# Forgetting attention: the values of a head in one run of 64-column products instead of two mixed runs

## The chip, the core and the metric

The kernel runs on one core of one Trainium2 chip. Time is device time in microseconds (us) of one launch; the kernel before takes 1184.59 us as the median of three runs (1183.14 to 1188.25). One further execution was recorded by the hardware profiler; its rows are what is read below. TensorE is called PE there (PEld is its weight load), VectorE DVE, ScalarE ACT, GpSimd POOL, and SyncE SP, whose queue issues most DMAs.

## The reference

Two layers on x of 1024 tokens by 1024 features. Layer 0 mixes a causal pooling branch with a cross-attention into 256 memory tokens; layer 1 mixes forgetting attention (16 heads of 64 features) with the same kind of memory attention. Each layer ends with a gated output projection, a residual and a LayerNorm. The change concerns the forgetting attention, cut here to its core:

```python
logits = einsum('bqhd,bkhd->bhqk', q, k) * scale + (cum_q - cum_k)
logits = where(kpos <= qpos, logits, -inf)
p = softmax(logits, axis=-1)
out = einsum('bhqk,bkhd->bqhd', p, v)          # "the values"
y = concat([out * silu(g_main), y_mem * silu(g_mem)]) @ w_out
```

## The kernel before, in words

All arithmetic that needs float32 accuracy is done with split operands: a number is a high part and a low part in 16 bits, and a product is the sum of three matmuls (high by high, high by low, low by high).

Layer 1's attention runs in the function `fox`. It goes through 16 heads, and in each through eight steps, one for each tile of 128 queries, the largest tile first: step 0 takes tile 7 (1024 keys wide, since the mask is causal), step 7 takes tile 0 (128 keys). A step has these parts on PE, in an order that the program fixes by hand: the logits of the tile (L323, one or two PSUM banks of the ring "L"), then a share of "fill" (the projections of queries, keys, values and gates for the heads to come, L359, whose columns are handed out so that the steps are equally long), then, in some steps, the values of older tiles (L1130), then the rest of the fill. On DVE the mask and the minimum are taken of the logits (L1068), on ACT the exponential (L1076), then ACT and DVE make the high and low halves of the probabilities (L1104 and L1105), and a transposing DMA from the SP queue (L1121) turns them, so that keys lie on the partitions. Tiles 3 and 2 go in one such DMA, and so do tiles 1 and 0. The turned tiles lie in six buffers of the tag "T".

Values are taken by `values(hd, c, o)`, six steps (LAG) behind the last of four tiles: tiles 7 to 4 (c = 1) in step 1 of the next head, tiles 3 to 0 (c = 0) in its step 5. A call has two parts. "Highs" take the high half of the probabilities with 128 stationary columns (the high and the low part of v side by side), 26 matmuls for c = 1 and 10 for c = 0. "Lows" take the low half with only the high part of v, which is 64 columns; two of them stand side by side in the array and write to the two halves of the partitions. c = 1 does its lows first, c = 0 its highs. The result lies in two halves of the partitions that must be added: ACT scales one half into the output tile `o` (L1148), DVE multiplies and adds the other (L1149). The bank is one of the four of the ring "L", which the logits use too. The table VALUES tells the fill how many columns the two steps spend on values, 39 and 15 blocks of 128.

After the second head of a pair, `pair_out` multiplies by the gate on POOL (L1158), right behind each call of `values`, and after c = 0 stores the pair to DRAM from the SP queue (L1160). The POOL queue also holds the masks of coming tiles (L1042) and the splitting of weights (L176, L193, L178).

The rest of the kernel uses the same eight PSUM banks: four "L", two "pj" (projections) and two "T" (exponentials, transposes).

Of the kernel before, what the change touches and what calls it, by code (L numbers as in the profile page):

```python
# [9 lines left out]
F32 = mybir.dt.float32  # L10
F32R = mybir.dt.float32r
BF16 = mybir.dt.bfloat16
F16 = mybir.dt.float16
# [25 lines left out]
QKSCALE = 2.0 ** -17  # L39
VALUES = {1: 39 * P, 5: 15 * P}  # L40

# [37 lines left out]
def trunk_kernel(ctx, tc, x, xT, memT, win, wk, wv0, wv, wmk, wmv, wout, poolw, pscale, lng, lnb, bforget, out):  # L79
# [15 lines left out]
    nc.vector.memset(warm, 0.0)  # L95
    idle = psum.tile([P, NH], F32, tag="L", name="idle", bufs=4)
    for _ in range(9):
# [30 lines left out]
    def w_slots(tags, where):  # L128

        def tiles(k):  # L130
            tag, bufs = tags[k]
            if tag == "w":
                return [parts_of(wt, [P, NH]) for _ in range(2)]
            two, four = [P, 2, NH], [P, 2, 2, NH]
            if tag == "MK":
                hi, pair = MK(two), MK(four, BF16)
            elif tag == "PG":
# [323 lines left out]
    def mem_attention(l, X, kv, qtile, ytile, yd, behind=None, before=None, last=None):  # L461
# [12 lines left out]
        if l:  # L474
            with tc.manual_schedule(engines={PE}):
                one, two = queries(0, ("L", 4)), queries(1)
# [19 lines left out]
        def probs(i):  # L496

            p, two = sb([P, MH, NMEM], "P", 4), sb([P, 2, MH, NMEM], "P", 4, F16)
            m, ms, sm, r = tiny(MH), tiny(MH), tiny(MH), tiny(MH)
            for hp in range(2):  # L500
                lg = ps([P, 2, NMEM], "L", 4)
                for n, j in ((0, 0), (0, 1), (1, 1), (2, 1), (1, 0), (2, 0)):
                    h = 2 * hp + j
                    a, b = three(qs[h][:, i * P : (i + 1) * P], mk[:, h, :])[n]
                    nc.tensor.matmul(lg[:, j, :], a, b, start=(n, j) == (0, 0), stop=(n, j) == (2, 0))
                pair = slice(2 * hp, 2 * hp + 2)
                nc.vector.tensor_reduce(m[:, pair], lg, AX.X, ALU.max, negate=True)
                nc.vector.tensor_scalar(ms[:, pair], m[:, pair], MSCALE, None, ALU.mult)
                for j in range(2):
                    h = 2 * hp + j  # L510
                    nc.scalar.activation(
                        p[:, h, :], lg[:, j, :], AF.Exp, bias=ms[:, h : h + 1], scale=MSCALE, accum_out=sm[:, h : h + 1],
                    )
            nc.vector.tensor_scalar(r, sm, 1.0 / PSCALE, None, ALU.mult)
            nc.vector.reciprocal(r, r)
            for h in range(MH):
                nc.scalar.activation(two[:, 0, h, :], p[:, h, :], AF.Copy, scale=r[:, h : h + 1])
                nc.vector.scalar_tensor_tensor(
                    two[:, 1, h, :], p[:, h, :], r[:, h : h + 1], two[:, 0, h, :], ALU.mult, ALU.subtract,
                )  # L520
            pt[i] = T([P, 2, MH, 2, P], F16)
            nc.sync.dma_start_transpose(
                pt[i].rearrange("p e h m q -> p (e h m) q"), two.rearrange("p e h t -> p (e h t)"),
            )

        def values(c, h):
            acc = ps([P, NH], *(("L", 4) if h == 1 else ("T", 2)))
            for j in range(4):
# [31 lines left out]
    class OutProj:  # L560
# [34 lines left out]

        def open(self, banks=(("L", 4), ("pj", 2)) * 2):
            accs = [ps([P, NH], *bank) for bank in banks]
            return accs[:2], accs[2:]
# [44 lines left out]
        def rest(self, resid, X, dst):  # L643
# [14 lines left out]
            for sp, c in order:  # L658
                if c == 2:
                    accs[sp] = self.open((("T", 2), ("T", 2), ("L", 4), ("L", 4))) if 0 in accs and sp == 1 else self.open()  # L660
                if self.begun and (sp, c) == (0, 0):
# [76 lines left out]
    with tc.tile_pool(name="in0", bufs=1) as in0:  # L738
# [34 lines left out]
        def pool_group(g, see=None):  # L773
            w = WINDOWS[g]
            pms = []
            for f in (2 * g, 2 * g + 1):
                u = sb([P, S], "P", 4)
                run(slab(
                    first[f] if g == 0 else win[0, f], X, lambda cols, acc: nc.scalar.copy(u[:, cols], acc),
                    ("L", 4) if f == 1 else ("pj", 2),  # L780
                ))
# [23 lines left out]
            for d in range(2):  # L805
                f = 2 * g + d
                for n in range(2):
                    acc = ps([P, NH], *(("pj", 2) if d and n else ("L", 4)))
                    terms = []
# [26 lines left out]
    with tc.tile_pool(name="in1", bufs=1) as in1:  # L836
# [9 lines left out]
        def vt(shape, dt=F32R):  # L846
            return sb(shape, "V", 4, dt, in1)

# [54 lines left out]
        def forget_gates():  # L903
# [23 lines left out]
            yield  # L927
            ca = ps([P, 2 * P], "L", 4)
            nc.tensor.matmul(ca[:, :n], tri, lf, start=True, stop=False)
# [122 lines left out]
        def probs(hd, i, R, sums, inverse, behind):  # L1052
# [11 lines left out]
            for n, (lo, up) in enumerate(parts):  # L1064
                lg = ps([P, NH], "L", 4)[:, : up - lo]
                mm3(lg, ((q[:, qs], kx[:, lo:up]), (q[:, qs], ky[:, lo:up])))
# [40 lines left out]

        pt = {}

        def turn(hd, i, two):  # L1110

            n = 2 * i + 2
            if i in (3, 1):
                joined.append(two)
                return
            to = T([P, 2 * ST, P], F16)
            pt[hd, i] = to
# [3 lines left out]
            nc.sync.dma_start_transpose(to[:, :n, :], two[:, : n * P])  # L1121
# [52 lines left out]
        def fox(following, out_proj, head):  # L1174
            fill, past, fresh = Fill(), [None] * LAG, [None]

# [6 lines left out]
            for hd in range(HEADS + 1):  # L1183
# [16 lines left out]
                for i in range(ST if hd < HEADS else LAG):  # L1200
                    tile_of = ST - 1 - i
                    last = ST + LAG if hd == HEADS else (hd | 1) * ST + ST
                    at = ST if hd == HEADS else hd * ST
                    todo = [VALUES.get(k % ST, 0) if k >= ST else 0 for k in range(at + i, last)]
# [64 lines left out]
        mem_attention(1, X, kv, xy, lambda: vt([P, S], F32), y1d[2], islice(own, 24), own_weights, first_weights)  # L1269
        fg = G((P, 8, ST * HEADS))  # L1270
# [69 lines left out]
```

## Time and profile before

| | |
|---|---|
| median of three runs | 1184.59 us (1183.14 to 1188.25) |
| profiled execution, its own time | 1185.35 us |
| its span, first to last instruction | 1183.5 us |
| mean granted TensorE clock | 0.996 |
| busy: PE, PEld | 1162.4 us (98%), 671.5 us (57%) |
| busy: DVE, ACT, POOL | 781.6 us (66%), 684.5 us (58%), 287.2 us (24%) |
| the `fox` stage | from about 643 us to 1056 us of the span |

A row of the list of groups reads: line, engine, operation, tiles (out<-in, buffer numbers left out), shapes, count, then busy time and mean duration of one, then the engine's idle time just ahead of them and what ended it. A row of the timeline reads: start, length, engine, line, operation, tiles, count, and in brackets an idle time ahead of it. Consecutive instructions of one line stand in one row. Matmuls are pipelined, so a row's length reaches past the start of the next row; what a run of matmuls occupies is read from its start to the next row's start.

### The profile page before, as it was taken

The numbers are of one execution on the slowest core, as the hardware profiler recorded it, in microseconds if no ns is written. First come the engines' busy times: TensorE is split into PE (matmuls) and PEld (weight loads), VectorE is DVE, ScalarE is ACT, GpSimd is POOL, SyncE is SP. The second block draws the span as 40 slices with busy tenths as digits, with TensorE's granted clock in tenths as the row PEclk, the third lists the DMA queues.
The fourth block names the chain that finished last, engine by engine and source line by source line (L and its number), as shares of the span: only waits on it lengthen the run. The fifth ranks groups of instructions, "written<-read, shape, count | busy, mean of one in ns | idle before, by whom it ended". The sixth has DMA issues, their size and how long they took to land. (4 is left out here: it accounts for less than half of the span.)

```text
span 1183.5 us, 19786 instructions
## 1 busy us (share of the span) xinstructions
PE 1162.4 (98%) x6894; PEld 671.5 (57%) x6941; DVE 781.6 (66%) x1841; ACT 684.5 (58%) x1514; POOL 287.2 (24%) x441
## 2 busy tenths in 40 slices
PE   8999999999999999999999999999999999999996
PEld 5566766555555557556674555555555555455553
DVE  6754675555766566457655888778777787874654
ACT  6578775976563234567421776667766767674120
POOL 3322001310000000000012454555555444750000
PEclk9999999999999999999999999999999999999998
DMA  7576647754385654446734889989997999875430
GB/s 258 182 249 192 168 103 213 247 179 148 92 276 160 160 143 122 136 137 114 189 134 114 179 193 211 194 174 197 201 211 147 169 196 204 216 184 177 153 132 36
DMA packets 286196, 203.89 MB, mean 172 GB/s; under 512 B 224912, under 2 KB 238352, under 8 KB 286096
## 3 DMA queue, kind: packets, MB, share of 16 engines
q1 hardware_dynamic: 279120, 179.49, 60.7%
q0 software_dynamic: 6976, 23.14, 6.0%
q8 instruction: 54, 0.88, 0.3%
q14 instruction: 46, 0.38, 0.1%
HBM read 116.01 MB, written 22.61 MB: 117 GB/s over the span
## 5 line engine op out<-in xcount | busy, mean ns | idle before, releaser
L359 PE MATMUL pj<-A,w 128*128 128x512 f16 (+2 forms) x2827 | 650.9, 383 | 2.1 <-DVE s L1089 0.5
L359 PEld LDWEIGHTS <-w 128*128 128x128 f16 (+1 forms) x2560 | 245.3, 98 | 277.9 <-issue 8.8
L1076 ACT ACTIVATE T<-MK,s 128x512 f32<-128x512 f32 x192 | 111.2, 579 | 67.0 <-DVE s L1068 50.0
L1105 DVE SCALAR_TENSOR_TENSOR P<-T,s,P 128x512 f16<-128x512 f32 x192 | 112.1, 613 | 39.1 <-ACT P L1104 38.0
L1104 ACT ACTIVATE P<-T,s 128x512 f16<-128x512 f32 x192 | 103.1, 576 | 53.3 <-issue 28.9
L615 PEld LDWEIGHTS <-T 128*128 128x128 bf16 x736 | 70.5, 98 | 88.4 <-issue 4.7
L1042 POOL TENSOR_SCALAR_AFFINE_SELECT raw<-R 128x256 f32<-128x256 f32 (+3 forms) x128 | 59.8, 469 | 179.4 <-DVE s L1068 97.9
L199 DVE TENSOR_TENSOR w<-raw,w 128x512 bf16<-128x512 f32 x74 | 52.0, 703 | 58.3 <-ACT w L198 39.8
L323 PE MATMUL L<-A 128*128 128x512 f16 (+3 forms) x384 | 84.1, 326 | 2.8 <-DVE G L1149 2.1
L556 POOL DMA_DIRECT2D y1d<-V x4 | 2.1, 535 | 337.2 <-DMA B<-in_wk_dram 331.3
L359 PEld LDWEIGHTS pj<-A,w 128*128 128x128 f32 x352 | 65.1, 188 | 16.8 <-ACT w L198 1.2
L199 DVE TENSOR_TENSOR T<-T,T 128x1024 bf16<-128x1024 f32 x22 | 26.8, 1220 | 68.1 <-PE pj L615 34.7
L178 POOL TENSOR_TENSOR w<-B,w 128x512 f16<-128x512 f32 x54 | 62.9, 1165 | 4.0
L323 PEld LDWEIGHTS <-A 128*128 128x128 f16 x384 | 37.3, 98 | 45.5 <-issue 4.0
L198 ACT CAST w<-raw 128x512 fp32r<-128x512 f32 x76 | 46.8, 615 | 24.3 <-DMA raw<-in_win_dram 10.2
L198 ACT CAST T<-T 128x1024 fp32r<-128x1024 f32 x22 | 23.0, 1047 | 63.4 <-DMA T<-y1d 32.9
L1130 PEld LDWEIGHTS <-V 128*64 128x64 f16 (+1 forms) x1152 | 50.8, 104 | 13.7 <-issue 6.2
L1130 PE MATMUL L<-T,V 128*64 128x128 f16 (+1 forms) x1152 | 57.5, 220 | 0.8 <-DVE s L1068 0.7
L615 PE MATMUL pj<-B,T 128*128 128x512 bf16 (+1 forms) x187 | 52.1, 385 | 0.3
L615 PE MATMUL L<-B,T 128*128 128x512 bf16 (+1 forms) x183 | 52.1, 393 | 0.2
L1068 DVE CUSTOM_DVE_ANT_0 MK<-L,R,scales 128x512 f32<-128x512 f32 x64 | 45.3, 707 | 8.2 <-PE L L323 8.0
L200 ACT CAST w<-raw 128x512 bf16<-128x512 f32 x78 | 48.2, 618 | 3.3 <-PE pj L359 1.9
(290 smaller groups left out, 1850.8 us busy)
## 6 DMA issues: line engine op xcount, KB each, us to landing
raw<-in_win_dram SPq DMA_DIRECT2D x66, 256.0 KB, 3.5
W<-in_win_dram POOLq DMA_DIRECT2D x48, 256.0 KB, 4.4
R<-cumd SPq DMA_DIRECT2D x16, 512.0 KB, 4.6
B<-in_win_dram SPq DMA_DIRECT2D x15, 512.0 KB, 5.3
y0d<-Y SPq DMA_DIRECT2D x12, 512.0 KB, 4.0
raw<-in_wout_dram SPq DMA_DIRECT2D x24, 256.0 KB, 2.7
T<-y0d SPq DMA_DIRECT2D x12, 512.0 KB, 4.4
A<-A SPq DMA_DIRECT2D x24, 256.0 KB, 3.9
```

The source lines that it names most:

```text
L178: pin(nc.gpsimd.tensor_tensor(to.lo, src, to.hi, ALU.subtract))
L198: pin(nc.scalar.copy(to.hi, src))
L199: pin(nc.vector.tensor_tensor(to.lo, src, to.hi.bitcast(F32), ALU.subtract))
L200: pin((top or nc.scalar.copy)(to.top, src))
L323: nc.tensor.matmul(acc, a, b, start=i == 0, stop=i == len(terms) - 1)
L359: nc.tensor.matmul(accs[n], a[:, k, :], b[:, pc * 4 + k, n * NH : (n + 1) * NH], start=seen[n] == 1, stop=seen[n] == 3 * KT,)
L615: nc.tensor.matmul(accs[a][nh], y, w, start=kt == 8 and i == 0, stop=kt == 7 and i == 2,)
L1042: tc.keep_in_program_order(nc.gpsimd.affine_select(C[:, :w], R[:, lo:up], [[-1, w]], ALU.is_ge, -NEG, base=w - P, channel_multiplier=1,))
L1076: nc.scalar.activation(e, p[:, lo:up], AF.Exp, bias=top, scale=-1.0, accum_out=sums[:, n, hd % 2, i : i + 1],)
L1104: nc.scalar.activation(pair[:, lo:up], e, AF.Copy, scale=r)
L1105: nc.vector.scalar_tensor_tensor(pair[:, L + lo : L + up], e, r, pair[:, lo:up], ALU.mult, ALU.subtract)
L1130: nc.tensor.matmul(acc[rows, (i % 4) * P : (i % 4) * P + P], v[:, b, 2 * j : 2 * j + (1 if e else 2), :].rearrange("p e d -> p (e d)"), pt ...
```

## The change

Heads 0 to 13 take their values in one call, `all_values`, in step 4 of the next head, four steps after the step in which their last tile is handed to the transposing DMA. It makes 108 matmuls of 64 columns (36 blocks by the three products of the split), 54 on each half of the partitions: tiles 7, 4, 3, 0 on one half, 6, 5, 2, 1 on the other, so that both halves are complete sums and nothing has to be added. Each half is scaled out once: the half that lies on the output's own partitions by DVE, the other by ACT. Heads 14 and 15 keep the old two calls.

The accumulator gets a bank of its own ("O"), and the ring "L" has three banks in place of four, everywhere in the kernel. Since all turned tiles of a head must live until its one run, the space is dealt anew: tile 5 goes to a separate buffer "U" for even heads (taken from "V", which has three buffers in place of four) and to unused rows of another tile for odd heads, there with two transposing DMAs in place of one; tiles 1 and 0 go behind tile 4 in its buffer. The gate products and the store of a pair are called two and three steps after the run. The buffers for the second output projection's weights are dealt in another order to fit.

```diff
-VALUES = {1: 39 * P, 5: 15 * P}
+SOON, FULL = 5, HEADS - 2
...
-                lg = ps([P, NH], "L", 4)[:, : up - lo]
+                lg = ps([P, NH], "L", 3)[:, : up - lo]
...
+        def values_at(k):
+
+            hd, i = divmod(k, ST)
+            if 0 < hd <= FULL:
+                return 54 * P if i == SOON - 1 else 0
+            return {1: 39 * P, 5: 15 * P}.get(i, 0) if hd > FULL else 0
...
-            to = T([P, 2 * ST, P], F16)
+            if i == 5 and hd <= FULL and hd % 2:
+                pt[hd, i] = to = lines[0][:, 7::8, : n * P // 2].rearrange("p e (j q) -> p e j q", q=P)
+                for e in range(2):
+                    nc.sync.dma_start_transpose(to[:, e], two[:, e * n * P // 2 : (e + 1) * n * P // 2])
+                return
+            if i == 5 and hd <= FULL:
+                to = ut([P, 2 * ST, P], F16)
+            elif i == 0 and hd < FULL:
+                to = late.pop(hd)[:, 10:, :]
+            else:
+                to = T([P, 2 * ST, P], F16)
+            if i == 4:
+                late[hd] = to
...
+        def all_values(hd, o):
+
+            v, un, b = pairs[hd // 2][2], unv if hd >= 4 else unv0, hd % 2
+            acc = ps([P, NH], "O", 1)
+            tiles = ((7, 4, 3, 0), (6, 5, 2, 1))
+            todo = [
+                [(i, j, e, f) for i in of for e, f in ((0, 0), (0, 1), (1, 0)) for j in range(i + 1)] for of in tiles
+            ]
+            for n in range(len(todo[0])):
+                for half, of in enumerate(tiles):
+                    i, j, e, f = todo[half][n]
+                    at = sorted(of).index(i) * P
+                    nc.tensor.matmul(
+                        acc[64 * half : 64 * half + 64, at : at + P], v[:, b, 2 * j + f, :],
+                        pt[hd, i][:, e, j] if len(pt[hd, i].shape) == 4 else pt[hd, i][:, e * (i + 1) + j, :], start=n == 0, stop=n == len(todo[0]) - 1,
+                    )
+            own = slice(64 * b, 64 * b + 64)
+            for half in range(2):
+                of = acc[64 * half : 64 * half + 64].rearrange("p (a r t) -> p a r t", a=2, r=2)
+                to = o[own].rearrange("p (a r t) -> p a r t", a=2, r=4)
+                to = to[:, :, 1:3, :] if half else to[:, :, 0::3, :]
+                if half == b:
+                    nc.vector.tensor_scalar(to, of, un[own], None, ALU.mult)
+                else:
+                    nc.scalar.activation(to, of, AF.Copy, scale=un[own])
...
-            acc = ps([P, NH], "L", 4)
+            acc = ps([P, NH], "O", 1)
...
+                    outs[:] = [(n - 1, *what) for n, *what in outs]
+                    while outs and outs[0][0] == 0:
+                        _, pair, c, of = outs.pop(0)
+                        pair_out(pair, c, of, gs.get(pair))
...
+                    done = past[LAG - SOON]
+                    if done and done[0] < FULL and done[1] == 0:
+                        all_values(done[0], done[2])
+                        if done[0] % 2:
+                            outs.extend((n, done[0] // 2, c, done[2]) for n, c in ((2, 1), (3, 0)))
...
-                    if older and older[1] % 4 == 0:
+                    if older and older[1] % 4 == 0 and older[0] >= FULL:
                         values(older[0], older[1] // 4, older[2])
...
-        wtags = [("B", 10), ("V", 4), ("MK", 4)] + [("B", 10)] * 3 + [("w", 0), ("MK", 4), ("R", 2), ("V", 4), ("PG", 0), ("B", 10)]
+        wtags = [("B", 10), ("B", 10), ("MK", 4), ("V", 3), ("B", 10), ("B", 10)] + [("w", 0), ("MK", 4), ("R", 2), ("VU", 0), ("PG", 0), ("B", 10)]
```

The diff does not show where the instructions land. The first place is DVE in head 3, around the scaling out of head 2's values. In the order before, P is a tile of probabilities, MK a masked tile of logits, G the output `o`, L a bank of logits or of values; L1068 (an ISA row) is the mask of one bank, L1149 adds tiles 7 to 4 of head 2 into `o`:

```order
L1068 ISA MK1200_7437,s1201_7438<-L1204_7446,raw1172_7326,s1201_7438,scales_108 128x384
L1068 ISA s1201_7438 128x1
L1089 RECIPROCAL s1203_7443<-s1203_7443 128x1
L1105 SCALAR_TENSOR_TENSOR P1205_7450<-T1193_7409,s1203_7443,P1205_7450 128x512
L1105 SCALAR_TENSOR_TENSOR P1205_7450<-T1194_7411,s1203_7443,P1205_7450 128x512
L1149 SCALAR_TENSOR_TENSOR G1105_7016<-L1209_7461,scales_108,G1105_7016 64x512
L1068 ISA MK1212_7523,s1213_7524<-L1214_7525,R1118_7057,scales_108 128x512
L1068 ISA s1213_7524 128x1
```

And in the order of the change, where L1171 scales out one half of all of head 2's values, and L1075 is the mask:

```order
L1112 SCALAR_TENSOR_TENSOR P1229_7634<-T1222_7605,s1228_7631,P1229_7634 128x384
L1112 SCALAR_TENSOR_TENSOR P1229_7634<-T1223_7607,s1228_7631,P1229_7634 128x256
L1171 TENSOR_SCALAR G1102_7048<-O1231_7641,scales_108 64x2x2x128
L1075 ISA MK1235_7762,s1236_7763<-L1237_7764,raw1204_7538,scales_108 128x384
L1075 ISA s1236_7763 128x1
```

What was between the masks of the two widest tiles (the row behind it masks a 512-wide part of tile 5) stands now behind the work on tile 4 and ahead of the mask of tile 2, in the narrow half of the head.

The second place is the SP queue in head 2 and at the start of head 3. Before (T is a buffer of turned tiles with 16, 14, 12, 10, 14 and 6 blocks of 128 for tiles 7, 6, 5, 4, 3 with 2, and 1 with 0; y1d is the store of pair 0):

```order
L1121 DMA_TRANSPOSE T1151_7221<-P1147_7205 128x12x128
L1121 DMA_TRANSPOSE T1160_7258<-P1158_7246 128x10x128
L1160 DMA y1d_114<-G949_6371 128x1024
L949 DMA A540_3341<-A540_3341 64x2048 x2
L1121 DMA_TRANSPOSE T1178_7347<-P1166_7279 128x14x128
L332 DMA B1651_9561<-in_wv_dram 128x2x512
L949 DMA A540_3341<-A540_3341 64x2048
L1121 DMA_TRANSPOSE T1196_7419<-P1184_7369 128x6x128
```

And in the change:

```order
L1147 DMA_TRANSPOSE U1147_7209<-P1143_7191 128x12x128
L1147 DMA_TRANSPOSE T1156_7348<-P1153_7230 128x10x128
L1212 DMA y1d_114<-G949_6371 128x1024
L956 DMA A540_3341<-A540_3341 64x2048 x2
L1147 DMA_TRANSPOSE T1173_7411<-P1162_7363 128x14x128
L1147 DMA_TRANSPOSE T1156_7348<-P1179_7435 128x6x128
L956 DMA A540_3341<-A540_3341 64x2048
L334 DMA B1624_9709<-in_wv_dram 128x2x512
```

The store keeps its place ahead of the last two transposing DMAs of the head; the last of these has moved ahead of two other transfers. In the odd heads that follow, tile 5 goes as two transfers of six blocks (L1133).

More of the change, by code (lines that the diff above doesn't have):

```diff
@@ L95, in trunk_kernel @@
     nc.vector.memset(warm, 0.0)
-    idle = psum.tile([P, NH], F32, tag="L", name="idle", bufs=4)
+    idle = psum.tile([P, NH], F32, tag="O", name="idle", bufs=1)
     for _ in range(9):
@@ L136, in tiles @@
                 hi, pair = MK(two), MK(four, BF16)
+            elif tag == "VU":
+                hi, pair = sb(two, "V", 3, F32R, where), sb(four, "U", 1, BF16, where)
             elif tag == "PG":
@@ L475, in mem_attention @@
             with tc.manual_schedule(engines={PE}):
-                one, two = queries(0, ("L", 4)), queries(1)
+                one, two = queries(0, ("L", 3)), queries(1)
                 run(islice(one, 24))
@@ L500, in probs @@
             for hp in range(2):
-                lg = ps([P, 2, NMEM], "L", 4)
+                lg = ps([P, 2, NMEM], "L", 3)
                 for n, j in ((0, 0), (0, 1), (1, 1), (2, 1), (1, 0), (2, 0)):
@@ L526, in values @@
         def values(c, h):
-            acc = ps([P, NH], *(("L", 4) if h == 1 else ("T", 2)))
+            acc = ps([P, NH], *(("O", 1) if h == 1 else ("T", 2)))
             for j in range(4):
@@ L594, in split, with open @@
                 self.n += 1
-        def open(self, banks=(("L", 4), ("pj", 2)) * 2):
+        def open(self, banks=(("L", 3), ("pj", 2)) * 2):
             accs = [ps([P, NH], *bank) for bank in banks]
@@ L659, in rest @@
                 if c == 2:
-                    accs[sp] = self.open((("T", 2), ("T", 2), ("L", 4), ("L", 4))) if 0 in accs and sp == 1 else self.open()
+                    accs[sp] = self.open((("T", 2), ("T", 2), ("L", 3), ("O", 1))) if 0 in accs and sp == 1 else self.open()
                 if self.begun and (sp, c) == (0, 0):
@@ L807, in pool_group @@
                 for n in range(2):
-                    acc = ps([P, NH], *(("pj", 2) if d and n else ("L", 4)))
+                    acc = ps([P, NH], *(("pj", 2) if d and n else ("L", 3)))
                     terms = []
@@ L846, in vt, with ut @@
         def vt(shape, dt=F32R):
-            return sb(shape, "V", 4, dt, in1)
+            return sb(shape, "V", 3, dt, in1)
+        def ut(shape, dt=F32R):
+            return sb(shape, "U", 1, dt, in1)
+        rows_in = [vt, vt, vt, ut]
         kv = mem_kv(1)
@@ L927, in forget_gates @@
             yield
-            ca = ps([P, 2 * P], "L", 4)
+            ca = ps([P, 2 * P], "O", 1)
             nc.tensor.matmul(ca[:, :n], tri, lf, start=True, stop=False)
@@ L1106, in halves @@
             return hd, i, pair
-        pt = {}
+        pt, late = {}, {}
+        def values_at(k):
[3 more added lines that the diff above has]
+            return {1: 39 * P, 5: 15 * P}.get(i, 0) if hd > FULL else 0
         def turn(hd, i, two):
@@ L1174, in fox @@
         def fox(following, out_proj, head):
-            fill, past, fresh = Fill(), [None] * LAG, [None]
+            fill, past, fresh, outs = Fill(), [None] * LAG, [None], []
             def two_lines(row):
@@ L1203, in fox @@
                     at = ST if hd == HEADS else hd * ST
-                    todo = [VALUES.get(k % ST, 0) if k >= ST else 0 for k in range(at + i, last)]
+                    todo = [values_at(k) for k in range(at + i, last)]
                     part = max(0, (fill.left + sum(todo)) / len(todo) - todo[0])
                     new, split = None, []
+                    outs[:] = [(n - 1, *what) for n, *what in outs]
+                    while outs and outs[0][0] == 0:
+                        _, pair, c, of = outs.pop(0)
+                        pair_out(pair, c, of, gs.get(pair))
                     def inverse():
```

4 lines of the change are left out of this document (2 added, 2 removed).

## The prediction

> **What bounds the kernel now.** I read the page's busy times first, then the waits of PE within the forgetting attention, then the timeline of one head.
>
> ```profile
> span 1183.5 us, 19786 instructions
> PE 1162.4 (98%) x6894; PEld 671.5 (57%) x6941; DVE 781.6 (66%) x1841; ACT 684.5 (58%) x1514; POOL 287.2 (24%) x441
> ```
>
> PE is busy for 98% of the span. So a change counts by what it does to PE: the time its matmuls occupy, and its waits. In the stage from 640 to 1060 us these are all that the view of waits has:
>
> ```profile
> PE L L323 <- DVE G L1149: 2.1, 3, 0.9
> PE L L1130 <- DVE s L1068: 0.7, 2, 0.4
> PE L L323 <- DVE s L1068: 0.7, 1, 0.7
> PE pj L359 <- DVE s L1089: 0.5, 1, 0.5
> PEld L1130 <- DMA T<-P: 0.6, 1, 0.6
> ```
>
> Of 420 us, 4.0 us are waits of PE for DVE, and one weight load waited 0.6 us for turned tiles. Logits waited 2.1 us because the values held one of the four banks until DVE had added them out. The rest must come from inside the runs of values, which the timeline shows for head 2's values in head 3:
>
> ```profile
> 712.28 0.92 PE L323 MATMUL L<-A 128*128 128x512 f16 x4
> 713.13 0.92 PE L1130 MATMUL L<-T,V 128*64 128x128 f16 x26
> 713.98 1.62 PE L1130 MATMUL L<-T,V 128*128 128x128 f16 x26
> 715.44 0.38 PE L359 MATMUL pj<-A,w 128*128 128x512 f16 x1
> ...
> 724.62 0.49 PE L323 MATMUL L<-A 128*128 128x384 f16 x2
> 724.94 0.81 PE L359 MATMUL pj<-A,w 128*128 128x512 f16 x3
> 725.59 1.12 PE L1130 MATMUL L<-T,V 128*128 128x128 f16 x20
> 726.24 0.47 PE L1130 MATMUL L<-T,V 128*64 128x128 f16 x10
> 726.65 1.04 PE L359 MATMUL pj<-A,w 128*128 128x512 f16 x4
> ```
>
> Read from start to next start. 26 highs take 715.44 - 713.98 = 1.46 us, 0.056 us each. 26 lows take 0.85 us, which is 13 pairs at 0.056 (0.73) and 0.12 more: two 64-column matmuls do run side by side, and the turn from 64 to 128 columns costs about 0.1 us. The logits ahead (two 512 wide, two 384 wide) take 0.85 us, where projections take 0.65 / 3 = 0.22 each and 384 columns 0.32 / 2 = 0.16: 0.76, so the turn into 64 columns costs 0.1 as well. The second run (its row of 20 holds the ten highs; the row of 10 shows where its lows start) takes 1.06 us for 15 places of 0.056 (0.84), 0.22 more for two turns. Thus a head pays 0.10 + 0.12 + 0.22 = 0.44 us for four turns.
>
> **The change, part by part.**
>
> *The run.* 108 matmuls of 64 columns are 54 pairs, 54 x 0.056 = 3.02 us, as many places as before (39 + 15). Two turns are left, 0.22 us. A head saves 0.44 - 0.22 = 0.22 us; 14 heads save 3.1 us. The pair's price is known from 13 pairs in a row and is used for 54. A lower price has no row. The other end is the average of the longest run, 52 matmuls in 2.31 us, 0.044 each: 108 would take 4.8 us in place of the 3.47 that the two old runs and their first turn take, 1.3 us more in each of 14 heads, 18.6 us in all. I take 0.056 for a pair, since all 13 hold it.
>
> *Scaling out.* Each head loses one of the two operations on ACT and one of the two on DVE:
>
> ```profile
> L1149 DVE SCALAR_TENSOR_TENSOR G<-L,scales,G 64x512 f32<-64x512 f32 x32 | 23.9, 748 | 3.9 <-ACT G L1148 2.9
> L1148 ACT ACTIVATE G<-L,scales 64x512 f32<-64x512 f32 x32 | 21.8, 682 | 1.1 <-PE L L1130 0.3
> L1158 POOL TENSOR_TENSOR G<-G,G 128x256 f32<-128x256 f32 x20 | 15.9, 817 | 18.9 <-DVE G L1149 18.9
> ```
>
> That is 14 x 0.75 = 10.5 us of DVE and 14 x 0.68 = 9.5 us of ACT. By itself it gives nothing, since PE's matmuls cover both engines (were DVE the path, it would be all of the 10.5 us), except where DVE's lateness reaches PE through the banks. There the place counts:
>
> ```profile
> 718.44 0.73 DVE L1149 SCALAR_TENSOR_TENSOR G<-L,scales,G 64x512 f32<-64x512 f32 x1
> 719.09 0.73 DVE L1068 CUSTOM_DVE_ANT_0 MK<-L,R,scales 128x512 f32<-128x512 f32 x1
> ...
> 719.22 0.38 PE L323 MATMUL L<-A 128*128 128x256 f16 x2 [0.27 <-DVE G L1149]
> ...
> 970.68 0.38 PE L323 MATMUL L<-A 128*128 128x256 f16 x2 [0.87 <-DVE G L1149]
> ...
> 1026.66 0.38 PE L323 MATMUL L<-A 128*128 128x256 f16 x2 [0.91 <-DVE G L1149]
> ```
>
> The three waits on L1149 lie in heads 3, 13 and 15. The first two go (0.27 + 0.87 = 1.1 us): the addition leaves the wide steps, and the values no longer borrow a logits bank. Head 15 still works on old-style values, so I let half of its 0.91 go (0.4). The 0.7 us in which values waited for a bank go too, since "O" is theirs alone, and of the 0.6 us for turned tiles I take 0.3, since the run starts later than tiles 7 to 4 need. Waits removed: 2.5 us, with 0 and 4.6 (all five rows) as ends.
>
> *Three banks for logits.* A logits matmul now waits for the mask three banks back, not four. What that costs is read by comparing its start with that mask's end. The tightest place is head 15, step 1:
>
> ```profile
> 1016.53 0.92 PE L323 MATMUL L<-A 128*128 128x512 f16 x4
> ...
> 1017.45 0.73 DVE L1068 CUSTOM_DVE_ANT_0 MK<-L,R,scales 128x512 f32<-128x512 f32 x1
> ```
>
> The second bank of this step starts two matmuls after 1016.53, at about 1016.96, and its bank three back (step 0's first) is masked until 1018.18: 1.2 us of new waiting. But DVE's lateness in this head is already paid further on, by the 0.7 us of L323 for the mask and the 0.91 at 1026.66; arriving later there, PE waits less. I add 0.5 us net, with 0 and 1.2 as ends here. Elsewhere the additions that made DVE late are gone from steps 1 to 3, so I add nothing; the far end is a rival.
>
> *Turned tiles.* The run needs tile 0 one step sooner than before. Head 2 is the tightest:
>
> ```profile
> 713.73 0.34 DVE L1105 SCALAR_TENSOR_TENSOR P<-T,s,P 128x128 f16<-128x128 f32 x1
> 715.77 1.69 SPq L1121 DMA_TRANSPOSE T<-P  x1
> 721.81 0.59 PE L323 MATMUL L<-A 128*128 128x512 f16 x2
> ...
> DMA to landing us min/median/max: 2.7/4.8/7.5
> ```
>
> Its last halves are ready at 714.1, the DMA is issued at 715.77 and lands at 720.6 by the median of these DMAs and at 723.3 by the longest. PE is through the logits of step 4 at 721.81 + 0.43 = 722.2, where the run would begin: a wait of 0 to 1.1 us; I take 0.5. The same order of queue holds the store of pair 0 ahead of it, as before. Tile 5 costs SP seven more transposing DMAs of 1.2 to 1.9 us (L1121's shortest and median issue); what is queued behind them is the next tiles, which have one to four steps. Nothing is added for them.
>
> *Gate products, stores.* The products (0.82 us, 20 of them) and the stores come later by one to five steps. POOL is busy 24% and sat idle 18.9 us waiting for L1149; its masks are covered better, not worse. The rest of the kernel loses a bank of "L" too:
>
> ```profile
> L505 PE MATMUL L<-MK,B 128*128 128x256 bf16 (+1 forms) x192 | 26.8, 295 | 0.0
> L615 PE MATMUL L<-B,T 128*128 128x512 bf16 (+1 forms) x183 | 52.1, 393 | 0.2
> ```
>
> The memory attention's logits and the output projections waited 0.0 and 0.2 us with four banks; the projection's next block needs a "pj" bank, of which there are two as before, ahead of its second "L". Nothing is taken.
>
> Sum: -3.1 - 2.5 + 0.5 + 0.5 = -4.6 us against the profiled 1185.35, which stands 0.76 above the median 1184.59; against the median, **1180.0 us**.
>
> **The rivals.**
>
> *Supply.* PE cannot be fed 216 instructions at the pair's rate. For it: no run in this trace is longer than 52 matmuls. Against it: the 26 lows show no slowing. Price as above, +18.6 for -3.1, with the other terms (-1.5): about 1201.7. It decides once a matmul takes over 0.030 us on the average (3.25 us for 108, where the turns' gain is used up). The Trainium skill, "TensorE: Matmul & The Clock Gate", section "Wait — 56ns, not 53.3ns?", states a floor of about 25 ns from start to start, and about 62 ns per MATMUL where the sequencer's code must decode each. By the first the run stays at 3.02 us, by the second it would take 6.7 us, an estimate; the 26 lows at 0.85 / 26 = 0.033 us lie between, and a run so short cannot tell them apart for 108.
>
> *Banks.* Three banks starve the logits. For it: wherever a bank was on loan, PE waited 0.3 to 0.9 us. If heads 1 to 15 each wait the mean of the three, 0.7 us, that is 10.5 us for the 2.1 of now: -3.1 + 8.4 = +5.3, slower, about 1189.9. It decides from (3.1 + 2.1) / 15 = 0.35 us a head. Against it: on loan the bank came together with the addition on DVE, which leaves.
>
> *Tiles too late.* The DMA engines, not PE, set the pace of the stage:
>
> ```profile
> 709.00:732.00 23.00, 22.73 (x168) 12.16 (x167) 18.58 (x57) 16.32 (x41) 12.99 (x20) 1.00 1.07 222
> 834.00:862.00 28.00, 28.00 (x193) 14.59 (x192) 22.68 (x66) 19.27 (x48) 13.66 (x22) 1.00 0.96 202
> ```
>
> Their share (the number before the last) is about all of the time. If half of the 14 runs wait 0.7 us for their last tile, 4.9 us, the gain is given back: 1184.9, no change. Against it: PE was 22.73 of 23.00 us busy in the same window, and only one load waited for tiles.
>
> **How the numbers follow.** The forecast has 0.63: 1180.0, by its ends 1176.5 to 1183. Supply has 0.08, banks 0.13, tiles 0.16. A measurement of this kernel tells a change from none at about 0.5%, 5.9 us: 1178.7 and 1190.5. The forecast falls below 1178.7 in 0.28 of all cases and between the two in 0.35; tiles fall between in 0.14 and beyond in 0.02; banks are half between (0.06), half beyond (0.07); supply is beyond (0.08). So faster 0.28, same 0.55, slower 0.17. The range goes down to the forecast's lower end and up to the banks' time: 1176 to 1190.
>
> **What would show it.** In the changed profile the values' rows should read 108 matmuls that take about 3.2 us from start to next start; 4.8 would be supply. The wait of L323 on L1149 should be gone but in head 15; waits of L on the mask above 3 us would be banks. Waits of the new run on DMA T<-P above 2 us would be tiles. A gain above 6 us would mean that the lighter DVE and ACT freed PE in places where this trace shows no wait.

## The result and the profile after

The changed kernel takes 1200.18 us in the median (1199.77 to 1200.83) beside 1186.18 us for the kernel before on the same chip: a ratio of 1.0123, 95% interval 1.0111 to 1.0134. It is **slower by 14 us**; 1180.0 had been forecast, with a range that ended at 1190.

Three groups of rows answer to those shown of before. First the page's busy times, then all that the view of PE's waits has for the forgetting attention (630 to 1080 us), where logits are now L325, projections L361, the output projection L617 and the mask L1075:

```profile
span 1198.1 us, 20781 instructions
PE 1163.5 (97%) x7398; PEld 671.2 (56%) x7445; DVE 775.0 (65%) x1827; ACT 677.4 (57%) x1500; POOL 288.0 (24%) x441
```

```profile
PE L L325 <- DVE s L1075: 14.8, 23, 1.9
PE pj L617 <- DVE G L378: 1.1, 1, 1.1
PE pj L361 <- DVE G L378: 0.5, 1, 0.5
```

and the timeline of PE around the run of values of head 9, in step 4 of head 10:

```profile
909.34 0.59 PE L325 MATMUL L<-A 128*128 128x512 f16 x2
909.87 1.42 PE L1161 MATMUL O<-T,V 128*64 128x128 f16 x43
...
912.07 1.00 PE L1161 MATMUL O<-T,V 128*64 128x128 f16 x30
913.01 0.50 PE L325 MATMUL L<-A 128*128 128x384 f16 x2
```

The reader is to see two things. The run does what it should: 108 matmuls from 909.87 to 913.01, 3.14 us. And PE, busy for about as long as before (1163.5 us for 1162.4), now waits for the mask 14.8 us in 23 places, where its waits in the stage of before were 4.0 us in all. DVE and ACT, which do less than before (775.0 and 677.4 us for 781.6 and 684.5), make PE wait more. In the timeline the stage, from the start of the first logits to that of the last, takes 410.2 us in place of 396.3, which is the loss.

Why DVE is late shows where it stands in its own queue. The first rows are DVE in head 10 before, the second the same place after; rows of one column are left out. MK<-L of 512 columns is the mask of tile 3, of 384 that of tile 2, of 256 that of tile 1. P<-T, two of 384 and 256 columns in one row, are the halves of tile 4; those of 512 ahead of them are of tile 5, and the one of 512 at the end is of tile 3:

```profile
904.75 0.73 DVE L1068 CUSTOM_DVE_ANT_0 MK<-L,raw,scales 128x512 f32<-128x512 f32 x1
...
905.64 1.14 DVE L1105 SCALAR_TENSOR_TENSOR P<-T,s,P 128x512 f16<-128x512 f32 x2
906.70 0.61 DVE L1068 CUSTOM_DVE_ANT_0 MK<-L,raw,scales 128x384 f32<-128x384 f32 x1
...
908.77 1.01 DVE L1105 SCALAR_TENSOR_TENSOR P<-T,s,P 128x384 f16<-128x384 f32 x2 [0.70 <-ACT P L1104]
...
910.96 0.48 DVE L1068 CUSTOM_DVE_ANT_0 MK<-L,raw,scales 128x256 f32<-128x256 f32 x1
...
912.46 0.74 DVE L1105 SCALAR_TENSOR_TENSOR P<-T,s,P 128x512 f16<-128x512 f32 x1
```

```profile
911.25 0.75 DVE L1075 CUSTOM_DVE_ANT_0 MK<-L,raw,scales 128x512 f32<-128x512 f32 x1
...
912.10 1.14 DVE L1112 SCALAR_TENSOR_TENSOR P<-T,s,P 128x512 f16<-128x512 f32 x2
...
915.22 1.01 DVE L1112 SCALAR_TENSOR_TENSOR P<-T,s,P 128x384 f16<-128x384 f32 x2 [0.70 <-ACT P L1111]
916.15 0.61 DVE L1075 CUSTOM_DVE_ANT_0 MK<-L,raw,scales 128x384 f32<-128x384 f32 x1
...
918.83 0.75 DVE L1112 SCALAR_TENSOR_TENSOR P<-T,s,P 128x512 f16<-128x512 f32 x1 [0.22 <-ACT P L1111]
...
920.09 0.48 DVE L1075 CUSTOM_DVE_ANT_0 MK<-L,raw,scales 128x256 f32<-128x256 f32 x1
```

Before, the mask of tile 2 stood **ahead** of the halves of tile 4: 1.95 us behind the mask of tile 3. After, it stands **behind** them: 4.90 us. Its logits are there by 913.5 (two matmuls of 384 columns from 913.01), and DVE is idle for the 0.70 us ahead of 915.22 in which it waits for ACT; but the mask is next in line only behind the halves. The next mask, of tile 1, has fallen back as well: it stood 6.21 us behind the mask of tile 3 and ahead of the halves of tile 3, and stands now 8.84 us behind it, after those halves. ACT takes the exponentials and needs the masks for them. Over the stage it waits 59.1 us for them (the second row, after) in place of 50.0:

```profile
ACT T L1076 <- DVE s L1068: 50.0, 43, 4.2
ACT T L1083 <- DVE s L1075: 59.1, 44, 2.8
```

Head 10 is one of two kinds. In nine heads (1 to 3, 6, 7 and 10 to 13) the mask of tile 2 has moved behind the halves of tile 4. In heads 4, 5, 8, 9 and 14 it stood there before already; in 4, 8 and 14 it is now behind the halves of tile 3 too. The distance from the mask of tile 3 to that of tile 2 has grown by 2.2 to 3.3 us in twelve of these 14 heads, and by 0.5 us in heads 5 and 9.

### The profile page after: what moved, and what is told of

Read it like the earlier page. It is cut to its first block, busy times and chain, and to the rows that moved or that the text cites. A ratio compares the mean times of both kernels' runs of the same rounds, so it can differ in the third digit from the quotient of the medians.

```text
span 1198.1 us, 20781 instructions
## 1 busy us (share of the span) xinstructions
PE 1163.5 (97%) x7398; PEld 671.2 (56%) x7445; DVE 775.0 (65%) x1827; ACT 677.4 (57%) x1500; POOL 288.0 (24%) x441
## 5 line engine op out<-in xcount | busy, mean ns | idle before, releaser
L361 PE MATMUL pj<-A,w 128*128 128x512 f16 (+2 forms) x2827 | 645.8, 383 | 2.8 <-DVE G L378 0.5
L361 PEld LDWEIGHTS <-w 128*128 128x128 f16 (+1 forms) x2560 | 246.8, 98 | 281.9 <-issue 10.5
L1083 ACT ACTIVATE T<-MK,s 128x512 f32<-128x512 f32 x192 | 110.9, 578 | 81.1 <-DVE s L1075 59.1
L617 PEld LDWEIGHTS <-T 128*128 128x128 bf16 x736 | 70.6, 98 | 87.5 <-issue 4.4
L325 PE MATMUL L<-A 128*128 128x512 f16 (+3 forms) x384 | 88.5, 326 | 15.5 <-DVE s L1075 14.8
L361 PEld LDWEIGHTS pj<-A,w 128*128 128x128 f32 x352 | 65.2, 188 | 16.5 <-DVE Y L378 0.9
L325 PEld LDWEIGHTS <-A 128*128 128x128 f16 x384 | 36.3, 98 | 62.2 <-issue 23.6
L617 PE MATMUL pj<-B,T 128*128 128x512 bf16 (+1 forms) x188 | 52.3, 385 | 0.2
L1075 DVE CUSTOM_DVE_ANT_0 MK<-L,R,scales 128x512 f32<-128x512 f32 x64 | 45.3, 708 | 5.7 <-PE L L325 5.7
L617 PE MATMUL L<-B,T 128*128 128x512 bf16 (+1 forms) x165 | 47.0, 395 | 0.2
L1161 PEld LDWEIGHTS <-V 128*64 128x64 f16 x1512 | 42.6, 110 | 5.9 <-issue 5.5
L1161 PE MATMUL O<-T,V 128*64 128x128 f16 x1260 | 44.9, 220 | 0.0
```

Source lines behind the costliest of these rows:

```text
L325: nc.tensor.matmul(acc, a, b, start=i == 0, stop=i == len(terms) - 1)
L361: nc.tensor.matmul(accs[n], a[:, k, :], b[:, pc * 4 + k, n * NH : (n + 1) * NH], start=seen[n] == 1, stop=seen[n] == 3 * KT,)
L617: nc.tensor.matmul(accs[a][nh], y, w, start=kt == 8 and i == 0, stop=kt == 7 and i == 2,)
L1083: nc.scalar.activation(e, p[:, lo:up], AF.Exp, bias=top, scale=-1.0, accum_out=sums[:, n, hd % 2, i : i + 1],)
L1161: nc.tensor.matmul(acc[64 * half : 64 * half + 64, at : at + P], v[:, b, 2 * j + f, :], pt[hd, i][:, e, j] if len(pt[hd, i].shape) == 4 el ...
```

## The experiments

Two theories stood first. **Banks**: three banks for logits are too few. **Place**: the run of 3.1 us in step 4 is longer than a step's equal share, so that the other steps, the wide ones 0 to 3 above all, are shorter on PE while DVE and ACT have as much to do in them. "Both" joins them. When these had fallen, a third, **Order**, took their place: the row of the mask in DVE's queue. Each group of runs had the kernel before beside it (1186.0 to 1186.5 us), and its ratios refer to that. The stage is from one profiled execution each.

| kernel | us, median | ratio to before, 95% interval | stage, us |
|---|---|---|---|
| before | 1186.2 | | 396.3 |
| the change | 1200.2 | 1.0123 (1.0111 to 1.0134) | 410.2 |
| before, three banks | 1188.1 | 1.0015 (1.0003 to 1.0027) | 398.4 |
| change, four banks | 1200.7 | 1.0128 (1.0112 to 1.0143) | 409.6 |
| change, fill moved to wide steps | 1199.1 | 1.0110 (1.0095 to 1.0125) | 406.5 |
| change, four banks and fill moved | 1199.1 | 1.0114 (1.0099 to 1.0129) | 405.9 |
| change, mask first | 1189.9 | 1.0034 (1.0022 to 1.0046) | 397.0 |
| change, run in step 5 | 1192.1 | 1.0058 (1.0037 to 1.0079) | 401.5 |
| change, mask first, four banks | 1190.7 | 1.0040 (1.0027 to 1.0054) | 396.2 |
| before, mask last | 1190.6 | 1.0044 (1.0029 to 1.0060) | 401.1 |
| mask first, tail | 1187.2 | 1.0007 (0.9997 to 1.0016) | 397.4 |
| mask first, tail, 512 columns of fill moved | 1184.0 | 0.9981 (0.9972 to 0.9990) | 394.6 |
| mask first, tail, 1024 columns moved | 1180.1 | 0.9950 (0.9933 to 0.9967) | 390.6 |
| the same with four banks | 1178.4 | 0.9941 (0.9924 to 0.9958) | 387.8 |

### The banks alone, before and after

Three banks put into the kernel before, and four put back into the change. The first takes all the lines on banks from the change's own diff, of which two are shown; the second has the same lines backwards:

```diff
-            acc = ps([P, NH], "L", 4)
+            acc = ps([P, NH], "O", 1)
-                lg = ps([P, NH], "L", 4)[:, : up - lo]
+                lg = ps([P, NH], "L", 3)[:, : up - lo]
```

> The kernel before with nothing changed but the banks: three for the logits, one of its own for the values (and the other uses of that bank as in the change). Theory Banks (what costs is that a logits matmul may run only three masks ahead): the loss of the change is all here, 1196 to 1200 us, with 10 to 14 us of waits of L on the mask in the forgetting attention. Theory Place (what costs is that the run of 3.1 us in step 4 is longer than a step's equal share, so that the other seven steps, the wide ones 0 to 3 among them, get less PE work while DVE and ACT have as much to do in them): the steps keep their lengths here, so 1184 to 1188 us. Theory Both (the shorter wide steps make DVE late, and the missing bank makes the lateness count): the trace of before has nine places where the start of the logits lies 0.2 to 1.2 us ahead of the end of the mask three banks back, 5.4 us in sum; less the 2.8 us of waits for a bank on loan, 1186 to 1190 us.

> The changed kernel with four banks that logits and values share, as before; the run, its place and its scaling stay. Banks: the loss is gone, 1180 to 1184 us. Place: the wide steps are as short as in the change, so DVE and ACT still set the pace there, 1194 to 1199 us. Both: most of the loss is gone, 1181 to 1186 us, and DVE stays 1 to 3 us later behind the logits than before.

Measured: 1188.1 and 1200.7 us. The missing bank costs the kernel before 2 us (0.4 to 3.2 by the interval), which is what Both had said, and giving it back to the change gains nothing, which none of the three had said. Banks falls. The waits only move: with four banks it is no longer the logits but the projections that wait.

```profile
PE pj L361 <- DVE A L960: 10.0, 8, 2.4
PE pj L361 <- DVE G L378: 3.4, 2, 3.1
PE L L325 <- DVE s L1075: 0.8, 2, 0.6
```

What stays is the pace of DVE. These are the first masks of heads 10, 11 and 12, in the change and in the change with four banks:

```profile
899.24 0.74 DVE L1075 CUSTOM_DVE_ANT_0 MK<-L,R,scales 128x512 f32<-128x512 f32 x1
...
924.52 0.74 DVE L1075 CUSTOM_DVE_ANT_0 MK<-L,R,scales 128x512 f32<-128x512 f32 x1
...
948.64 0.74 DVE L1075 CUSTOM_DVE_ANT_0 MK<-L,R,scales 128x512 f32<-128x512 f32 x1
```

```profile
900.14 0.74 DVE L1075 CUSTOM_DVE_ANT_0 MK<-L,R,scales 128x512 f32<-128x512 f32 x1
...
925.42 0.74 DVE L1075 CUSTOM_DVE_ANT_0 MK<-L,R,scales 128x512 f32<-128x512 f32 x1
...
949.54 0.74 DVE L1075 CUSTOM_DVE_ANT_0 MK<-L,R,scales 128x512 f32<-128x512 f32 x1
```

25.28 and 24.12 us in both. With three banks or four, DVE and ACT go through a pair of heads in 49.40 us, and PE follows. Before, it was 47.87 (the same masks stood at 891.20, 915.66 and 939.07), where PE's own work for a pair is 45.8.

### Fill moved to the wide steps

A number is added to what steps 5 to 7 are thought to work, so that less fill goes to them and more to steps 0 to 3 (and, in a second kernel, four banks too):

```diff
+        def spare(k):
+            return 8 * P if k % ST > 4 and k // ST <= FULL else 0
...
-                    todo = [values_at(k) for k in range(at + i, last)]
+                    todo = [values_at(k) + spare(k) for k in range(at + i, last)]
```

> The changed kernel, three banks, but steps 5, 6 and 7 count 1024 columns more than they work, so that the fill goes from them (0.25 us less each) to steps 0 to 3 (0.19 us more each); the total of the fill is the same. Banks: the waits move but stay, 1197 to 1201 us. Place: the wide steps are as long as before, 1184 to 1189 us. Both: 1188 to 1195 us.

> Four shared banks and the fill moved to the wide steps. Banks: no better than the four banks alone, 1180 to 1184 us. Place: no better than the moved fill alone, 1184 to 1189 us. Both: no wait is left to speak of, 1178 to 1182 us.

Measured: 1199.1 us each. The first lies in the range of Banks, which the four banks had ruled out; for the second all three were wrong. Place falls as a cause of its own, and so does Both: with the fill back in the wide steps and as many banks as before, the kernel is as slow. So neither PE's steps nor its banks set the pace.

### The mask first, or the run elsewhere

An edge that orders two instructions on one engine and adds no other wait puts the mask of tile 2 ahead of the halves of tile 4 (kept in `held`) on DVE. PE's order is fixed by the program; DVE, ACT and POOL are ordered by a planner, and with the edge in place it moved two more things: the mask of tile 1 went ahead of the halves of tile 3 (in 11 of the heads 2 to 14), and ACT's scaling out ahead of the exponential of tile 3 (in heads 2 to 14). So the run tests the order of these rows together and not the one mask alone:

```diff
-                nc.vector.tensor_tensor_reduce(p[:, lo:up], lg, rows, unq, top, ALU.add, ALU.min, m[:, n : n + 1])
+                ins = nc.vector.tensor_tensor_reduce(p[:, lo:up], lg, rows, unq, top, ALU.add, ALU.min, m[:, n : n + 1])
+                if i == 2 and 0 < hd <= FULL:
+                    for old in held.pop(hd):
+                        tc.add_manual_dep(old.ins, ins.ins.name, mybir.DependencyInfo(mybir.DependencyClass.NoSync, mybir.DependencyReason.DATA), reason="mask first")
```

> The changed kernel with one thing put back: in heads 1 to 14 the mask of tile 2 stands ahead of the two halves of tile 4 on DVE, as in the kernel before (in the change it stands behind them). Every instruction, the run, its place and the three banks stay. Theory Order (the run pushed this mask behind the halves in the queue of DVE, so that DVE and ACT work through tiles 4 to 2 one after the other instead of side by side, and a head takes them 25.27 and 24.13 us where PE needs 22.9): most of the loss goes, 1181 to 1188 us, and the distance from the mask of tile 3 to that of tile 2 falls from 4.8 to 5.6 us to below 4 us. Theory Place (the run itself shortens the other steps): no change, 1197 to 1201 us.

> The mask of tile 2 first, and four shared banks. Order: the order decides and the banks add little, within 3 us of the run with the order alone. Place: as slow as the four banks alone, 1198 to 1202 us.

A third kernel leaves the planner alone and moves the run (`SOON, FULL = 6, HEADS - 2`):

> The changed kernel with the run one step later, in step 5, behind the logits of tile 2; the order on DVE has the mask of tile 2 ahead of the halves of tile 4 again, and now the mask of tile 1 (256 wide) behind the halves of tile 3 and the scaling. Order: a smaller serial piece, 1184 to 1193 us. Place: the run is as long and the other steps as short, 1196 to 1201 us.

And a fourth does the reverse to the kernel before: the mask of tile 2 is held behind the halves of tile 4, and nothing else is edited. The place changes in the nine heads where it stood ahead of them.

> The kernel before, with its two old runs of values, its four banks and all its steps, but the mask of tile 2 held behind the halves of tile 4 on DVE in heads 1 to 14, as the change has it. Order: the loss comes without the change, 1193 to 1200 us. Place: 1184 to 1189 us.

Measured: 1189.9 us with the mask first, 10.3 us of the 14 gone. DVE in head 10 now reads

```profile
908.62 0.75 DVE L1075 CUSTOM_DVE_ANT_0 MK<-L,raw,scales 128x512 f32<-128x512 f32 x1
...
909.47 1.14 DVE L1115 SCALAR_TENSOR_TENSOR P<-T,s,P 128x512 f16<-128x512 f32 x2
...
911.85 0.62 DVE L1075 CUSTOM_DVE_ANT_0 MK<-L,raw,scales 128x384 f32<-128x384 f32 x1
```

3.23 us from mask to mask in place of 4.90, and the heads 10 and 11 take DVE 24.07 and 22.91 us (first masks at 896.60, 920.67 and 943.58) in place of 25.28 and 24.12: 1.2 us less for each. The distance is below 4 us in heads 2 to 14, as Order had said, and 5.15 in head 1. In heads 4, 5, 8, 9 and 14 the mask stands ahead of the halves where the kernel before has it behind, so this order is not quite that of before. The time was just above what Order had expected (1188), so something is left, below.

Four banks on top of it change nothing (1190.7), as Order said. With the run in step 5 the mask of tile 2 stands ahead of or behind the halves of tile 4 in the same heads as before the change, and the mask of tile 1 stands behind the halves of tile 3, in head 10 behind the scaling out too:

```profile
911.10 0.61 DVE L1075 CUSTOM_DVE_ANT_0 MK<-L,raw,scales 128x384 f32<-128x384 f32 x1
...
915.16 1.27 DVE L1112 SCALAR_TENSOR_TENSOR P<-T,s,P 128x512 f16<-128x512 f32 x2 [0.22 <-ACT P L1111]
...
916.47 0.76 DVE L1171 TENSOR_SCALAR G<-O,scales 64x512 f32<-64x512 f32 x1
917.26 0.48 DVE L1075 CUSTOM_DVE_ANT_0 MK<-L,raw,scales 128x256 f32<-128x256 f32 x1
```

The mask of tile 1 (256 columns) comes 6.16 us behind that of tile 2, where it was 4.26 in the kernel before. 1192.1 us: the masks that fall back are those whose logits stand behind the run. The reverse, in the kernel before, costs 1190.6 - 1186.0 = 4.6 us, less than Order had said (7 to 14). 2.0 us of the waits of PE's matmuls there are for weights that POOL splits, and the kernel before has no such wait of a matmul. It moves one mask in nine heads, where the change moves the masks of tiles 2 and 1 and the scaling out on ACT; four banks and the older shares of fill stay as well. Which of these makes up the difference was not taken apart. So the order of DVE's rows makes a loss without the change, and the order of DVE and ACT together is worth 10.3 us in it; the share of each moved row is open.

### What was left: the tail, and the fill once more

With the mask first the stage was about as long as before (397.0 us for 396.3), but behind its last logits PE waited for a bank of the output projection:

```profile
1047.08 0.63 PE L617 MATMUL L<-MK,B 128*128 128x512 f32 x2
1050.01 0.73 PE L617 MATMUL pj<-B,B 128*128 128x512 f32 x2 [2.30 <-DVE G L378]
1050.58 0.39 PE L617 MATMUL pj<-V,B 128*128 128x512 f32 x1
1050.90 0.30 PE L1187 MATMUL O<-T,V 128*64 128x128 f16 x4
```

The bank holds the last gate, which DVE takes late. In the kernel before, the old run of head 15 stands ahead of these matmuls (eleven of the projection's are ahead of it) and covers the delay; with the new shares of fill it stands behind fifteen. The next kernels bring it three matmuls forward, ahead of the wait again, and then move fill as before, with 0, 512 and 1024 columns, the last also with four banks:

```diff
+                    soon = 0.1 if (hd, i) == (HEADS, 1) else FRAC[0]
-                    fill.pump(part * FRAC[0])
+                    fill.pump(part * soon)
```

> The mask of tile 2 first, three banks, and behind the last head the old run of tiles 7 to 4 of head 15 three matmuls earlier, where the kernel before has it. In the run with the mask first alone, the output projection waited 2.3 us for a bank that the last gate (DVE L378) still held, and the values' run stood behind that wait. Theory Sum (the loss is the order on DVE, plus 2.3 us of this wait, plus the banks): 1185 to 1188 us, 2 us below that run. Rival (the last gate is late in any case and something else then waits for it): 1189 to 1191 us.

> The same, and steps 5 to 7 count 512 columns more than they work, which gives steps 0 to 3 about 0.1 us of fill each. Sum: the 6.6 us of waits of L on the mask in step 3 fall by half, 1182 to 1186 us. Rival (DVE and ACT, not PE, now set the length of a head, 24.06 and 22.9 us from mask to mask): no gain over the run without it.

> The same with 1024 columns, 0.19 us for each of steps 0 to 3. Sum: the waits of step 3 go, 1179 to 1184 us, which is the 3 us of the longer runs gained over the kernel before. Rival: no gain over the run without it, 1185 to 1190 us.

> All of this with four shared banks. Sum: as with three banks, 1179 to 1184 us, since no logits wait for a bank any more and the run itself now waits for one (3.3 us in the run with mask first and four banks). Rival: 1185 to 1190 us.

Measured: 1187.2, 1184.0, 1180.1 and 1178.4 us. Sum's times hold for the first three, and the fourth is 0.6 us below its range. Its account of the waits is rougher: with 512 columns the waits of logits on the mask went from 6.9 to 5.3 us, not by half, and with 1024 to 1.7. The first of these kernels cannot be told from the kernel before (1.0007, 0.9997 to 1.0016): within that, the order and the wait at the tail are the whole loss, and what the run saves shows only with the fill moved. The moved fill, worth 1 us while the order was wrong, is worth 7 once it is right. The kernel with all of it is the fastest of all, 0.9941 of before (0.9924 to 0.9958), and the view of PE's waits has no row left for the stage. The timeline of PE, its first logits of heads 12, 13 and 14, and then those of heads 10 and 12 of before, a pair without a wait:

```profile
936.38 1.03 PE L325 MATMUL L<-A 128*128 128x512 f16 x4
...
959.50 1.03 PE L325 MATMUL L<-A 128*128 128x512 f16 x4
...
981.75 1.03 PE L325 MATMUL L<-A 128*128 128x512 f16 x4
```

```profile
890.56 0.38 PE L323 MATMUL L<-A 128*128 128x512 f16 x1
...
936.38 0.38 PE L323 MATMUL L<-A 128*128 128x512 f16 x1
```

A pair of heads takes PE 45.37 us (heads 10 and 11: 45.36) in place of 45.82: 0.23 us less for each head, without a wait on either side. The stage is 8.5 us shorter than before. Of these, 14 heads at 0.23 are 3.2, and the waits of before are 4.0; the rest was not taken apart.

## Why the prediction was wrong

- **The run.** Right. 3.14 us and 0.10 us for the turn ahead (two logits of 512 columns take 909.87 - 909.34 = 0.53 us, 0.43 by themselves); 3.02 + 0.22 had been said. The saving of 0.22 us a head is the 0.23 that the last kernel shows. *Supply* was no danger.
- **Scaling out.** The amounts were right:

```profile
L1171 DVE TENSOR_SCALAR G<-O,scales 64x512 f32<-64x512 f32 x14 | 10.4, 743 | 1.5 <-ACT G L1173 1.4
L1173 ACT ACTIVATE G<-O,scales 64x512 f32<-64x512 f32 x14 | 9.5, 682 | 1.3 <-DVE G L1171 1.0
```

  14 rows on each engine, at the durations used, where there had been 28. "By itself it gives nothing" held too. The waits on the old additions went, worth 2.5 us by the forecast; 14.8 us of new ones came.
- **Three banks for logits.** By itself the missing bank costs about 2 us, where 0.5 had been said; the interval of 0.4 to 3.2 does not rule that out. I compared starts of logits with ends of masks as they stood in the trace of before, and "elsewhere the additions that made DVE late are gone" took it that DVE could only come earlier. The *Banks* rival told where the waits would be seen ("waits of L on the mask above 3 us") and priced them at 10.5 us; 14.8 came, but four banks do not remove the loss, so the mechanism was another.
- **Turned tiles.** No wait of the run for the tiles is in the trace; 0.5 us had been allowed. *Tiles too late* falls.
- **Gate products, stores** at 0: nothing in the runs speaks against it. **The rest of the kernel** at 0 missed the wait at the tail: 1.1 us in the change as it came, 2.3 with the mask first, and 2.8 us between the two runs that differ in it (1189.9 and 1187.2, of different groups).
- **The step that failed** is the one that put DVE and ACT at nothing: "By itself it gives nothing, since PE's matmuls cover both engines", and for the logits "so I add nothing". There is no term for what comes to stand behind the run on these two. "That is 14 x 0.75 = 10.5 us of DVE" counts work, and "cover" takes it that they go on beside PE. What the runs showed in its place is 14.8 us of PE's waits for the mask, of which the order of rows on DVE and ACT is the cause: 10.3 us came back with it. The engines had little to spare: a pair of short heads took DVE 47.87 us where PE's work is 45.8, and only the longer heads (4, 5, 8, 9 and 14, with gates among their fill, 28.1 us each) let it catch up. The order of the change that stands ahead of the prediction has it in its rows: both halves of tile 4, L1171, and only then the mask of 384 columns. But beside it stood rows of another step of the kernel before (its addition L1149 lies between the masks of tiles 6 and 5), and I read both for what was added and removed, not for what had changed places. Rows of before would have bounded it: there the halves of tile 4 end at 908.77 + 1.01 = 909.78, 5.0 us behind the start of the mask of tile 3, so a mask put behind them starts about 5.0 us after that mask and not 1.95. 4.90 was measured in head 10. With some 3 us later in one step of most of 14 heads, in two engines with little to spare in the short heads, the loss should have been a rival of its own.

The Trainium skill, "Perfetto Trace Analysis", section "Identifying the Most-Contended Engine", has it that for Vector and Scalar the share of busy time is a fair measure of how close they are to their roofline. By it both have room here, DVE at 65% of the span of the change and ACT at 57%, and nothing in the trace speaks against that. But the share does not show the chain between the two: 14.8 us of PE's waits end with DVE's mask, and a change of places in their queues, with the same instructions on both, gave back 10.3 us. The same skill, "PSUM — Partial Sum Buffer", section "Engine vs sequencer instructions", says that these engines' queues are strict first in, first out. The mask of tile 2 agrees with it: its operand was ready at 913.5, DVE was idle for the 0.70 us ahead of 915.22, and it started at 916.15.

That the planner turned the order *because* it takes the logits of tile 2 to come later is inferred from the run in step 5, where the mask of tile 2 keeps its old place; how the planner decides was not measured.

## What to carry to other kernels

When a change moves a long run on one engine, compare the order of all the other engines for rows that changed places, and price the chain between two engines that feed each other, not their busy time: here two engines at 65% and 57% set the pace. If a tuned kernel's loss does not answer to the resource that its waits name (a bank), look at whether the waits only move to another name while the releaser keeps its pace. An idea that is right may need its surroundings tuned again: the same run gave 1200 us as it came, and 1178 with the masks ahead again, one run three matmuls earlier, its fill dealt by what DVE needs, and four banks.

## What the runs showed of the hardware

108 matmuls of 64 columns, each with a weight load of its own, went at 3.14 / 108 = 0.029 us each, in each of the 14 heads that have such a run:

```profile
L1161 PEld LDWEIGHTS <-V 128*64 128x64 f16 x1512 | 42.6, 110 | 5.9 <-issue 5.5 <-DMA B<-in_wout_dram 0.4
```

A load took 110 ns, nearly four times the distance from one matmul to the next, and PE lost nothing by it: with two matmuls side by side, pairs keep their pace of 0.056 us (3.14 less 0.12 for the turn back, over 54 pairs) in a run of 216 instructions as they did in one of 52. The Trainium skill's floor of about 25 ns ("TensorE: Matmul & The Clock Gate", section "Wait — 56ns, not 53.3ns?") is near what is seen. Its 62 ns per MATMUL, which it states for hardware decode off, would have made the run 6.7 us, an estimate, and is not what bounded it here.
